# Row-wise log-sum-exp on one core: another middle range check, another division of the rows, 17 loads for 18

## The chip, the cores and the metric

The kernel runs on one core of a Trainium2 chip. The core has a tensor engine (PE), a vector engine (VectorE, DVE in the profile), a scalar engine (ScalarE, ACT), a general engine (GpSimd, POOL) and a queue engine (SyncE, SP) that issues transfers here. The metric is the time of one execution on the device in microseconds; lower is better. The time before the change is 162.31, the median of three runs (162.27 to 162.44).

## The reference

The input `x` is 32 x 512 x 1024 in 32-bit floats, drawn from a normal distribution. For each of the 16,384 rows of 1024 values the logarithm of the sum of exponentials is wanted:

```python
def reference(x):
    max_x = np.max(x, axis=-1, keepdims=True)
    return (max_x.squeeze(-1) + np.log(np.sum(np.exp(x - max_x), axis=-1))).astype(np.float32)
```

The input is 67.1 MB, the output 64 KB.

## The kernel before

Each of the 128 partitions takes 128 rows (112 from the first part of `x`, 16 from the rest), so "a row" below means one row of 1024 values on every partition at once. The kernel sums `exp(x)` without taking the maximum off. At the end it checks that every sum lies in a safe range (`LOW` 1e-15, total below `HIGH` 1e15). Only if not, a second, slow branch computes everything again with the maximum; on this input that branch is not entered.

**The list.** `LOADS` (line 23) is the plan, written out by hand. Each entry is one transfer: its size in rows, which may be a fraction, and how the rows that are complete with it are summed. SP issues the transfers in this order into `ring`, a buffer of 48 rows; a transfer into a part of the ring that was used waits until the engine that read it last is done (`load`, L132). ScalarE takes the exponential of each load in place (L213), in pieces when an entry has several parts.

**The kinds of rows.**
- `R`: VectorE reduces whole rows, several in one instruction (L224).
- `T`: VectorE adds the two halves of one row with `scalar_tensor_tensor`, whose accumulator gives the sum (`add_halves`, L156). It reads two inputs of 512 elements, one instruction and one accumulator read for each row.
- `G`: POOL adds the second half of the rows to the first (a fold, L219); later VectorE reduces the 512 elements left (`sum_folded`, L148). `H` says that the waiting folds are summed here; otherwise they are summed at the end of the entry.
- `a` and `b`: the last row comes in two pieces. `a` is summed by halves like `T`; `b` is summed by ScalarE itself, by the accumulator of its exponential (L208).
- `L`: ScalarE takes the logarithm of the first 112 sums (L199), which SP stores early (L245).
- `C`: the middle range check over the columns of `sumexp` filled so far (`check`, L163 and L167), with two matmuls that start the count in PSUM (L173, L174).

**The order.** Each engine has one queue, in the order in which the loop over `LOADS` writes it. Engines wait for each other by counting semaphores (`Counted`). `addr_align` (L186) stands on VectorE's queue ahead of the load number `ALIGNED` (15, counted from 0) and pads its instructions with empty ones up to an address boundary.

**The end.** When VectorE has its last sum and ScalarE the sum of `b`, two branches run. ScalarE takes the logarithm of 15 more columns (L249) and of the last, whose two pieces are added by the bias (L251); SP stores 16 columns (L255). Beside it VectorE checks the remaining columns (L163, L167), PE adds up over the partitions (L173, L174, L259), VectorE compares (L263), and ScalarE and VectorE read the verdict and branch.

Of the kernel before, what the change touches and what calls it, by code (L numbers as in the profile page):

```python
# [9 lines left out]
LOW, HIGH = 1e-15, 1e15  # L10
# [7 lines left out]

LOADS = [
# [4 lines left out]
]  # L26


# [23 lines left out]
def kernel(  # L52
# [5 lines left out]
    nc = tc.nc  # L58
# [43 lines left out]
    bad = sbuf("bad", 2)  # L102
    total = sbuf("total", 2)
# [31 lines left out]

    c = 0
    p = 0
    here = 0
    done_before = 0
    first_load = None  # L140
    folded = []
    summed = []

    def sum_folded():
        for c0, p0, s, at in folded:
            dve.wait(pool, at)
            half = ring[:, p0 : p0 + s * d].rearrange("p (c d) -> p c d", d=d)[:, :, 0:H]
            at = dve.did(nc.vector.reduce_sum(out=sumexp[:, c0 : c0 + s], in_=half, axis=AX.X))  # L148
            users.append((p0, p0 + s * d, dve, at))
            summed.append((c0, c0 + s, at))  # L150
        folded.clear()

    def add_halves(v, col):
        h = v.shape[-1] // 2
        lo = v[:, 0:h]
        return dve.did(nc.vector.scalar_tensor_tensor(  # L156
            out=lo, in0=lo, scalar=1.0, in1=v[:, h : 2 * h],
            op0=ALU.mult, op1=ALU.add, accum_out=sumexp[:, col : col + 1],
        ))

    def check(k, c0, c1):
        dve.wait(dve, dve.n)
        dve.did(nc.vector.scalar_tensor_tensor(  # L163
            out=clamped[:, c0:c1], in0=sumexp[:, c0:c1], scalar=LOW, in1=sumexp[:, c0:c1],
            op0=ALU.max, op1=ALU.not_equal, accum_out=bad[:, k : k + 1],
        ))
        at = dve.did(nc.vector.reduce_sum(  # L167
            out=total[:, k : k + 1], in_=sumexp[:, c0:c1], axis=AX.X
        ))
        if k == 0:  # L170
            pe.wait(pool, constants)
        pe.wait(dve, at)
        pe.did(nc.tensor.matmul(count, lhsT=bad[:, k : k + 1], rhs=far, start=k == 0, stop=False))  # L173
        pe.did(nc.tensor.matmul(count, lhsT=ones, rhs=total[:, k : k + 1], start=False, stop=False))  # L174

    for i, (size, parts) in enumerate(loads):
        if here + size > RING * d:
            assert here == p
            p = here = 0
        dma = load(i, here, done_before, size)  # L180
        first_load = first_load or dma.ins
        end = here + size
        done_before += size
        act.wait(landed[i], 16)
        if i == ALIGNED:
            nc.vector.addr_align(128)  # L186
        for k, part in enumerate(parts):
            if part[0][0] == "H":
                sum_folded()
                continue  # L190
            if part[0][0] == "C":
                sum_folded()
                checked = c
                check(0, 0, c)
                continue
            if part[0][0] == "L":
                assert c >= W
                act.wait(dve, max(at for c0, _, at in summed if c0 < W))
                ln_early = act.did(nc.scalar.activation(  # L199
                    out=res[:, 0:W], in_=sumexp[:, 0:W], func=AF.Ln  # L200
                ))
                continue
            rows = sum(s for how, s in part if how in "RTG")
            more = any(q[0][0] not in "HLC" for q in parts[k + 1 :])
            upto = p + rows * d if more else end
            v = ring[:, here:upto]
            if part[-1][0] == "b":
                last = act.did(nc.scalar.activation(  # L208
                    out=v, in_=v, func=AF.Exp, accum_out=sumexp[:, NC : NC + 1]
                ))  # L210
                here = upto
                continue
            at = act.did(nc.scalar.activation(out=v, in_=v, func=AF.Exp))  # L213
            here = upto
            for how, s in part:
                rows = ring[:, p : p + s * d].rearrange("p (c d) -> p c d", d=d)
                if how == "G":
                    pool.wait(act, at)
                    folded.append((c, p, s, pool.did(nc.gpsimd.tensor_tensor(  # L219
                        out=rows[:, :, 0:H], in0=rows[:, :, 0:H], in1=rows[:, :, H:d], op=ALU.add,  # L220
                    ))))
                elif how == "R":
                    dve.wait(act, at)
                    users.append((p, p + s * d, dve, dve.did(nc.vector.reduce_sum(  # L224
                        out=sumexp[:, c : c + s], in_=rows, axis=AX.X
                    ))))
# [12 lines left out]
                p += s * d  # L239
        sum_folded()  # L240
        assert here == end
    assert c == LAST
    assert sorted(q for c0, c1, _ in summed for q in range(c0, c1)) == list(range(NC))
# [5 lines left out]
    act.did(nc.scalar.activation(out=res[:, W:LAST], in_=sumexp[:, W:LAST], func=AF.Ln))  # L249
    act.wait(act, last)  # L250
    ln_last = act.did(nc.scalar.activation(  # L251
        out=res[:, LAST:NC], in_=sumexp[:, NC : NC + 1], func=AF.Ln, bias=sumexp[:, LAST:NC]
    ))
    sp.wait(act, ln_last)
    nc.sync.dma_start(out=out_rest, in_=res[:, W:NC]).then_inc(stored, 16)  # L255

    check(1, checked, NC)
    pe.wait(act, last)
    at = pe.did(nc.tensor.matmul(  # L259
        count, lhsT=ones, rhs=sumexp[:, NC : NC + 1], start=False, stop=True  # L260
    ))
    dve.wait(pe, at)
    at = dve.did(nc.vector.tensor_scalar(out=fine, in0=count, scalar1=HIGH, scalar2=None, op0=ALU.is_lt))  # L263
# [6 lines left out]
    with nc.If(all_fine < 1):  # L270
# [5 lines left out]
        for c0 in range(0, NC, RING):  # L276
            s = min(RING, NC - c0)
            v = ring[:, 0 : s * d].rearrange("p (c d) -> p c d", d=d)
# [4 lines left out]
            for c1, c2 in ((c0, edge), (edge, c0 + s)):  # L283
                if c1 == c2:
                    continue
                nc.scalar.dma_start(
                    out=ring[:, (c1 - c0) * d : (c2 - c0) * d],
                    in_=source(c1 * d, (c2 - c1) * d),
# [4 lines left out]
                out=neg, in_=v, op=ALU.max, axis=AX.X, negate=True  # L293
# [3 lines left out]
                out=v, in0=v, in1=neg[:, :, None].to_broadcast([P, s, d])  # L297
# [5 lines left out]
                out=sumexp[:, c0 : c0 + s], in_=v, axis=AX.X  # L303
# [71 lines left out]
```

## Time and profile before

| | before |
|---|---|
| median of 3 runs, us | 162.31 (162.27 to 162.44) |
| profiled execution, us | 162.29 |
| its span, us | 161.0 |
| VectorE busy | 119.1 us, 74% |
| ScalarE busy | 115.0 us, 71% |
| POOL busy | 32.4 us, 20% |
| PE busy | 0.5 us |
| HBM read | 67.11 MB, 417 GB/s over the span |

The span runs from the first to the last instruction of one profiled execution; the execution's time has 1.3 more around it. A row of the order of time begins with the start and the length in microseconds, then engine, line, operation, and output and input with their shapes; what stands in brackets is how long the engine stood idle before and what ended it. A row of the groups has the busy time in microseconds, then the mean in nanoseconds, then the idle time before. Lengths of neighbours on one engine overlap a little, so the cost of one in a busy queue is the distance between two starts.

### The profile page before, as it was taken

To read this page: it belongs to the slowest core of one execution; us is meant where nothing else is said; L and a number is where in the kernel's file an instruction comes from. 1 tells how busy PE (TensorE), PEld (TensorE's weight loads), DVE (VectorE), ACT (ScalarE), POOL (GpSimd) and SP (SyncE) were. 2 spreads that over 40 slices of the span, in tenths; PEclk is the share of its full clock that TensorE was granted. 3 is DMA by queue.
4 is the path that set the end of the run, shared out by engine and by line. 5 is a ranking of instruction groups with operands and counts; after the bars stand their busy time and mean duration, and the time that the engine had idled before them with its cause. 6 is when DMAs were issued, how large, how long until landed. Compare 5 with 4: busy or idle time off the path is not lost.

```text
span 161.0 us, 202 instructions
## 1 busy us (share of the span) xinstructions
PE 0.5 (0%) x10; PEld 0.3 (0%) x10; DVE 119.1 (74%) x48; ACT 115.0 (71%) x32; POOL 32.4 (20%) x15
## 2 busy tenths in 40 slices
PE   0000000000000000000000000000000000000000
PEld 0000000000000000000000000000000000000000
DVE  0000000019999499995999999999999999999996
ACT  3000059980799609994199938996997999799995
POOL 0000000000000000000008800006950806737700
DMA  7996996996996996996999969899997999999991
GB/s 261 521 521 261 521 521 261 521 521 261 521 521 261 521 521 261 521 521 261 495 469 469 469 294 507 378 401 469 455 455 336 448 420 450 390 435 412 425 409 33
DMA packets 2882, 67.18 MB, mean 417 GB/s; under 512 B 577, under 2 KB 577, under 8 KB 1345
## 3 DMA queue, kind: packets, MB, share of 16 engines
q1 hardware_dynamic: 2880, 67.18, 97.4%
q14 instruction: 2, 0.01, 0.0%
HBM read 67.11 MB, written 0.07 MB: 417 GB/s over the span
## 4 chain that ended last, share of the span: by engine, by line
DVE 52%; DMA 30%; ACT 12%; POOL 4%; issue 1%; DVEq 0%; PE 0%
DVE sumexp L224 38%; DMA ring<-in_x_dram 30%; ACT ring L213 12%; DVE sumexp L148 10%; POOL ring L219 4%; DVE ring L156 3%; DVE clamped L163 1%; DVEq L186 0%; DVE total L167 0%; PE count L173 0%; DVE fine L263 0%; PE count L259 0%; PE count L174 0%
## 5 line engine op out<-in xcount | busy, mean ns | idle before, releaser
L213 ACT ACTIVATE ring<-ring 128x16384 f32<-128x16384 f32 (+22 forms) x26 | 112.3, 4371 | 42.5 <-DMA ring<-in_x_dram 42.4
L224 DVE TENSOR_REDUCE sumexp<-ring 128x16 f32<-128x16384 f32 (+6 forms) x10 | 96.1, 9639 | 40.0 <-ACT ring L213 40.0
L219 POOL TENSOR_TENSOR ring<-ring 128x1024 f32<-128x1024 f32 (+5 forms) x9 | 32.1, 3579 | 118.3 <-ACT ring L213 118.3
L148 DVE TENSOR_REDUCE sumexp<-ring 128x2 f32<-128x1024 f32 (+5 forms) x9 | 16.1, 1802 | 0.4 <-POOL ring L219 0.4
L156 DVE SCALAR_TENSOR_TENSOR ring<-ring 128x512 f32<-128x512 f32 (+1 forms) x11 | 6.5, 642 | 0.0
L120 ACT ACT_TABLE_LOAD x1 | 1.3, 1283 | 1.4 <-PEq L61 1.4
L163 DVE SCALAR_TENSOR_TENSOR clamped<-sumexp 128x114 f32<-128x114 f32 (+1 forms) x2 | 0.9, 462 | 0.1
L208 ACT ACTIVATE ring<-ring 128x768 f32<-128x768 f32 x1 | 0.8, 843 | 0.1
L173 PE MATMUL count<-far,bad 128*1 128x1 f32 x4 | 0.4, 163 | 159.2 <-DVE total L167 159.2
L156 DVE DVE_READ_ACCUMULATOR ring<-ring 128x1 f32 x11 | 0.8, 76 | 0.0
L173 PEld LDWEIGHTS count<-far,bad 128*1 128x1 f32 x4 | 0.2, 80 | 159.2 <-POOL ring L219 151.1
L249 ACT ACTIVATE res<-sumexp 128x15 f32<-128x15 f32 x1 | 0.2, 216 | 0.4 <-DVE ring L156 0.4
L263 DVE TENSOR_SCALAR fine<-count 1x1 int32<-1x1 f32 x1 | 0.1, 147 | 0.4 <-PE count L259 0.4
L167 DVE TENSOR_REDUCE total<-sumexp 128x1 f32<-128x114 f32 (+1 forms) x2 | 0.4, 212 | 0.0
L174 PE MATMUL count<-total,ones 128*1 128x1 f32 x4 | 0.4, 163 | 0.0
L121 POOL MEMSET ones<- 128x1 f32 x1 | 0.1, 98 | 1.0 <-POOLq L61 1.0
L199 ACT ACTIVATE res<-sumexp 128x112 f32<-128x112 f32 x1 | 0.3, 280 | 0.0
L251 ACT ACTIVATE res<-sumexp 128x1 f32<-128x1 f32 x1 | 0.3, 279 | 0.0
L174 PEld LDWEIGHTS count<-total,ones 128*1 128x1 f32 x4 | 0.2, 81 | 0.0
L259 PE MATMUL count<-sumexp,ones 128*1 128x1 f32 x2 | 0.2, 163 | 0.0
L208 ACT ACTIVATION_READ_ACCUMULATOR ring<-ring 128x1 f32 x1 | 0.2, 186 | 0.0
L163 DVE DVE_READ_ACCUMULATOR clamped<-sumexp 128x1 f32 x2 | 0.2, 79 | 0.0
(6 smaller groups left out, 0.6 us busy)
## 6 DMA issues: line engine op xcount, KB each, us to landing
ring<-in_x_dram SPq DMA_DIRECT2D x1, 7376.0 KB, 24.9
ring<-in_x_dram SPq DMA_DIRECT2D x1, 5936.0 KB, 19.6
ring<-in_x_dram SPq DMA_DIRECT2D x1, 4768.0 KB, 16.4
ring<-in_x_dram SPq DMA_DIRECT2D x1, 3520.0 KB, 15.1
ring<-in_x_dram SPq DMA_DIRECT2D x1, 2976.0 KB, 21.8
ring<-in_x_dram SPq DMA_DIRECT2D x1, 1792.0 KB, 27.4
ring<-in_x_dram SPq DMA_DIRECT2D x1, 1520.0 KB, 25.0
ring<-in_x_dram SPq DMA_DIRECT2D x1, 1360.0 KB, 19.2
```

The source lines that it names most:

```text
L120: nc.scalar.preload_act_table_set("natural_log_exp_and_others")
L148: at = dve.did(nc.vector.reduce_sum(out=sumexp[:, c0 : c0 + s], in_=half, axis=AX.X))
L156: return dve.did(nc.vector.scalar_tensor_tensor(out=lo, in0=lo, scalar=1.0, in1=v[:, h : 2 * h], op0=ALU.mult, op1=ALU.add, accum_out=sume ...
L163: dve.did(nc.vector.scalar_tensor_tensor(out=clamped[:, c0:c1], in0=sumexp[:, c0:c1], scalar=LOW, in1=sumexp[:, c0:c1], op0=ALU.max, op1=A ...
L167: at = dve.did(nc.vector.reduce_sum(out=total[:, k : k + 1], in_=sumexp[:, c0:c1], axis=AX.X))
L173: pe.did(nc.tensor.matmul(count, lhsT=bad[:, k : k + 1], rhs=far, start=k == 0, stop=False))
L174: pe.did(nc.tensor.matmul(count, lhsT=ones, rhs=total[:, k : k + 1], start=False, stop=False))
L199: ln_early = act.did(nc.scalar.activation(out=res[:, 0:W], in_=sumexp[:, 0:W], func=AF.Ln))
L208: last = act.did(nc.scalar.activation(out=v, in_=v, func=AF.Exp, accum_out=sumexp[:, NC : NC + 1]))
L213: at = act.did(nc.scalar.activation(out=v, in_=v, func=AF.Exp))
L219: folded.append((c, p, s, pool.did(nc.gpsimd.tensor_tensor(out=rows[:, :, 0:H], in0=rows[:, :, 0:H], in1=rows[:, :, H:d], op=ALU.add,))))
L224: users.append((p, p + s * d, dve, dve.did(nc.vector.reduce_sum(out=sumexp[:, c : c + s], in_=rows, axis=AX.X))))
```

## The change

- The list has 17 entries for 18. The first four and the first nine hold as many rows as before (64 and 112); the sizes from the fifth on differ.
- The third load is `R12+T4`: twelve rows reduced whole, four by halves. Over the whole list there are 86 `R` rows (89 before), 18 `T` rows (10) and 21 `G` rows (28) in five folds (nine).
- The new kind `A`: ScalarE takes the exponential of one row and its sum by the accumulator, one instruction for each row. Two rows of the ninth load (`G4 A2 R1`) are summed so.
- The middle check `C` is now two reductions with one input, the least and the total of the columns so far. They go into two columns of `sumexp` behind the sums (`LEAST`, `TOTAL`); `b` has its own column behind them (`REST`). The closing check reads the columns since `C` together with `LEAST`, and adds them together with `TOTAL`. PE has three matmuls at the end and none in the middle.
- `L` stands in the tenth entry, `C` in the eleventh; before, `C` stood in the tenth and `L` in the twelfth.
- `ALIGNED` stays 15, which is now the entry before the last.

```diff
 LOADS = [
-    (16, "R16"), (16, "R16"), (16, "R16"), (16, "G6 H R10"), (14.40625, "R9 G5"),
-    (11.59375, "G3 R5 R4"), (9.3125, "G3 H R6"), (6.875, "G4 R3"), (5.8125, "G2 H R4"),
-    (2.96875, "G2 C"), (3.5, "G2 H T2"), (2.65625, "G1 T2 L"), (1.46875, "T1"),
-    (1.6875, "T2"), (1.28125, "T1"), (0.9375, "T1"), (0.75, "T1+a"), (0.75, "b"),
+    (16, "R16"), (16, "R16"), (16, "R12+T4"), (16, "R11 G5"), (11.21875, "G5 H R6"),
+    (12.78125, "R7 R6"), (9.625, "R7 G2"), (8.34375, "G5 R3"), (6.03125, "G4 A2 R1"),
+    (4.53125, "R1+T3 L"), (3.28125, "T3 C"), (2.59375, "T3"), (1.875, "T2"),
+    (1.34375, "T1"), (0.96875, "T1"), (0.6875, "T1+a"), (0.71875, "b"),
 ]
...
-    sumexp = sbuf("sumexp", NC + 1)
+    LEAST, TOTAL, REST = NC, NC + 1, NC + 2
+    sumexp = sbuf("sumexp", NC + 3)
...
-    def check(k, c0, c1):
+    def check_early(c):
+        dve.wait(act, summed_by_act)
         dve.wait(dve, dve.n)
-        dve.did(nc.vector.scalar_tensor_tensor(
-            out=clamped[:, c0:c1], in0=sumexp[:, c0:c1], scalar=LOW, in1=sumexp[:, c0:c1],
-            op0=ALU.max, op1=ALU.not_equal, accum_out=bad[:, k : k + 1],
-        ))
-        at = dve.did(nc.vector.reduce_sum(
-            out=total[:, k : k + 1], in_=sumexp[:, c0:c1], axis=AX.X
-        ))
-        if k == 0:
-            pe.wait(pool, constants)
-        pe.wait(dve, at)
-        pe.did(nc.tensor.matmul(count, lhsT=bad[:, k : k + 1], rhs=far, start=k == 0, stop=False))
-        pe.did(nc.tensor.matmul(count, lhsT=ones, rhs=total[:, k : k + 1], start=False, stop=False))
+        for op, col in ((ALU.min, LEAST), (ALU.add, TOTAL)):
+            dve.did(nc.vector.tensor_reduce(
+                out=sumexp[:, col : col + 1], in_=sumexp[:, 0:c], op=op, axis=AX.X
+            ))
...
+            if part[0][0] == "A":
+                assert here == p
+                for _ in range(part[0][1]):
+                    v = ring[:, p : p + d]
+                    summed_by_act = act.did(nc.scalar.activation(
+                        out=v, in_=v, func=AF.Exp, accum_out=sumexp[:, c : c + 1]
+                    ))
+                    users.append((p, p + d, act, summed_by_act))
...
-    check(1, checked, NC)
+    dve.wait(act, summed_by_act)
+    dve.wait(dve, sums)
+    dve.did(nc.vector.scalar_tensor_tensor(
+        out=clamped[:, 0 : LEAST + 1 - checked], in0=sumexp[:, checked : LEAST + 1], scalar=LOW,
+        in1=sumexp[:, checked : LEAST + 1], op0=ALU.max, op1=ALU.not_equal, accum_out=bad,
+    ))
+    at = dve.did(nc.vector.reduce_sum(
+        out=total, in_=sumexp[:, checked : TOTAL + 1], axis=AX.X
+    ))
+    pe.wait(pool, constants)
+    pe.wait(dve, at)
+    pe.did(nc.tensor.matmul(count, lhsT=bad, rhs=far, start=True, stop=False))
+    pe.did(nc.tensor.matmul(count, lhsT=ones, rhs=total, start=False, stop=False))
```

More of the change, by code (lines that the diff above doesn't have):

```diff
@@ L98 @@
     ring = sbuf("ring", RING * d)
-    sumexp = sbuf("sumexp", NC + 1)
+    LEAST, TOTAL, REST = NC, NC + 1, NC + 2
+    sumexp = sbuf("sumexp", NC + 3)
     res = sbuf("res", NC)
     clamped = sbuf("clamped", NC)
-    bad = sbuf("bad", 2)
-    total = sbuf("total", 2)
+    bad = sbuf("bad", 1)
+    total = sbuf("total", 1)
     far = sbuf("far", 1)
@@ L142 @@
     summed = []
+    summed_by_act = 0
+    by_act = 0
     def sum_folded():
@@ L193 @@
                 checked = c
-                check(0, 0, c)
+                check_early(c)
                 continue
@@ L197 @@
                 assert c >= W
+                assert dve.seen[act.sem.num] >= summed_by_act
                 act.wait(dve, max(at for c0, _, at in summed if c0 < W))
@@ L201 @@
                 ))
+                continue
+            if part[0][0] == "A":
[6 more added lines that the diff above has]
+                    users.append((p, p + d, act, summed_by_act))
+                    by_act += 1
+                    c += 1
+                    p += d
+                    here += d
                 continue
@@ L208 @@
                 last = act.did(nc.scalar.activation(
-                    out=v, in_=v, func=AF.Exp, accum_out=sumexp[:, NC : NC + 1]
+                    out=v, in_=v, func=AF.Exp, accum_out=sumexp[:, REST : REST + 1]
                 ))
@@ L242 @@
     assert c == LAST
-    assert sorted(q for c0, c1, _ in summed for q in range(c0, c1)) == list(range(NC))
+    assert by_act + sum(c1 - c0 for c0, c1, _ in summed) == NC
     sp.wait(act, ln_early)
@@ L251 @@
     ln_last = act.did(nc.scalar.activation(
-        out=res[:, LAST:NC], in_=sumexp[:, NC : NC + 1], func=AF.Ln, bias=sumexp[:, LAST:NC]
+        out=res[:, LAST:NC], in_=sumexp[:, REST : REST + 1], func=AF.Ln, bias=sumexp[:, LAST:NC]
     ))
@@ L255 @@
     nc.sync.dma_start(out=out_rest, in_=res[:, W:NC]).then_inc(stored, 16)
-    check(1, checked, NC)
+    dve.wait(act, summed_by_act)
[11 more added lines that the diff above has]
+    pe.did(nc.tensor.matmul(count, lhsT=ones, rhs=total, start=False, stop=False))
     pe.wait(act, last)
     at = pe.did(nc.tensor.matmul(
-        count, lhsT=ones, rhs=sumexp[:, NC : NC + 1], start=False, stop=True
+        count, lhsT=ones, rhs=sumexp[:, REST : REST + 1], start=False, stop=True
     ))
```

## The prediction

> **What bounds the kernel now.** I read the chain that ended last, then busy time by stage, then the order of time at the end, then the mean durations by shape. All times are microseconds from the start of the span. The chain's shares come first:
>
> ```profile
> DVE 52%; DMA 30%; ACT 12%; POOL 4%; issue 1%; DVEq 0%; PE 0%
> ```
>
> The stages are cut at the first fold's sum, at the ninth load's landing and at the last landing. The columns are PE, PEld, DVE, ACT and POOL busy time, then the clock, the DMA share and GB/s:
>
> ```profile
> 0.00:92.02 92.02, 0.00 (x0) 0.00 (x0) 51.66 (x4) 55.02 (x6) 7.07 (x7) 1.00 0.99 427
> 92.02:138.01 45.99, 0.00 (x0) 0.00 (x0) 45.99 (x10) 39.05 (x10) 16.13 (x4) 1.00 1.00 430
> 138.01:157.75 19.74, 0.24 (x4) 0.16 (x4) 19.71 (x27) 19.63 (x14) 9.21 (x5) 1.00 0.98 408
> 157.75:161.00 3.25, 0.29 (x6) 0.18 (x6) 1.70 (x10) 1.33 (x4) 0.00 (x0) 1.00 0.04 5
> ```
>
> The DMA never rests before 157.75, and from 92.02 VectorE does not either (45.99 of 45.99, 19.71 of 19.74). So there are two bounds, and the end shows by how much they differ:
>
> ```profile
> 157.75 0.84 ACT L208 ACTIVATE ring<-ring 128x768 f32<-128x768 f32 x1
> 158.14 0.68 DVE L156 SCALAR_TENSOR_TENSOR ring<-ring 128x512 f32<-128x512 f32 x1
> 158.50 0.19 ACT L208 ACTIVATION_READ_ACCUMULATOR ring<-ring 128x1 f32 x1
> 158.75 0.28 DVE L156 SCALAR_TENSOR_TENSOR ring<-ring 128x128 f32<-128x128 f32 x1
> 158.97 0.07 DVE L156 DVE_READ_ACCUMULATOR ring<-ring 128x1 f32 x1
> 159.07 0.22 ACT L249 ACTIVATE res<-sumexp 128x15 f32<-128x15 f32 x1 [0.39 <-DVE ring L156]
> 159.07 0.17 DVE L163 SCALAR_TENSOR_TENSOR clamped<-sumexp 128x14 f32<-128x14 f32 x1
> 159.50 0.34 SPq L255 DMA_DIRECT2D out_dram<-res  x1
> 159.72 0.15 DVE L263 TENSOR_SCALAR fine<-count 1x1 int32<-1x1 f32 x1 [0.38 <-PE count L259]
> ```
>
> ScalarE has finished the last load at 158.69 and waits 0.39 for VectorE's last sum. That sum starts both branches of the end: the closing logarithms with the last store, and the closing range check. After 159.07 nothing in either branch changes length (PE still has its three closing matmuls), so what the change is worth is how much earlier than 159.07 those two instructions start. With VectorE out of the way, ScalarE could start at about 158.72: 0.35, plus what the last landing moves.
>
> **The loads.** ScalarE started at once on landing three times, which gives the landings:
>
> ```profile
> 21.80 13.86 ACT L213 ACTIVATE ring<-ring 128x16384 f32<-128x16384 f32 x1 [19.07 <-DMA ring<-in_x_dram]
> ...
> 79.85 13.95 ACT L213 ACTIVATE ring<-ring 128x6144 f32<-128x6144 f32 x2 [5.48 <-DMA ring<-in_x_dram]
> ...
> 138.01 1.75 ACT L213 ACTIVATE ring<-ring 128x1856 f32<-128x1856 f32 x1 [0.91 <-DMA ring<-in_x_dram]
> ```
>
> Three loads of 16 rows took 58.05, so 1.2094 a row. From 138.01 to 157.75 sixteen rows in nine loads took 19.74, where 16 x 1.2094 is 19.35: 0.043 more for each load. In both kernels the first nine loads hold 112 rows, so load 9 (of the new 17) still lands at 138.01. The eight after it take 19.35 + 8 x 0.043 = 19.69 and the last lands at 157.70, 0.05 earlier. The DMA must not run dry for that. The tightest row is
>
> ```profile
> ring<-in_x_dram SPq DMA_DIRECT2D x1, 4768.0 KB, 16.4
> ```
>
> whose own transfer takes 9.31 x 1.2094 = 11.3, so it was issued 5.1 before its turn. In the new list the tightest is the sixth load, which waits for the twelve rows of the third: issued at about 87.4 for a turn at 93.4, six to spare. No wait of SP becomes tight.
>
> **VectorE.** Its prices:
>
> ```profile
> L224 DVE TENSOR_REDUCE sumexp<-ring 128x16 f32<-128x16384 f32 x3 | 51.7, 17219 | 40.0 <-ACT ring L213 40.0
> L224 DVE TENSOR_REDUCE sumexp<-ring 128x4 f32<-128x4096 f32 x2 | 8.8, 4409 | 0.0
> L148 DVE TENSOR_REDUCE sumexp<-ring 128x5 f32<-128x2560 f32 x1 | 2.8, 2808 | 0.0
> L219 POOL TENSOR_TENSOR ring<-ring 128x2560 f32<-128x2560 f32 x1 | 5.6, 5624 | 17.9 <-ACT ring L213 17.9
> L219 POOL TENSOR_TENSOR ring<-ring 128x2048 f32<-128x2048 f32 x1 | 4.5, 4537 | 5.5 <-ACT ring L213 5.5
> ```
>
> A row reduced whole costs (17.219 - 4.409) / 12 = 1.067, with about 0.06 for each instruction once its tail overlaps the next; a folded row half of that, 0.533. A row by halves (T) is 0.61, from the starts of the last two sums above (158.14, 158.75). POOL's fold is 1.09 a row.
>
> Four rows of the third load by halves save 4 x (1.067 - 0.61) = 1.8 there:
>
> ```profile
> 74.40 17.22 DVE L224 TENSOR_REDUCE sumexp<-ring 128x16 f32<-128x16384 f32 x1 [2.13 <-ACT ring L213]
> ...
> 92.02 3.35 DVE L148 TENSOR_REDUCE sumexp<-ring 128x6 f32<-128x3072 f32 x1 [0.40 <-POOL ring L219]
> ```
>
> The twelve end at 74.40 + 12.86 = 87.26, the four at 89.71. Load 4 now begins with eleven whole rows, whose exp ends at 79.85 + 9.59 = 89.44, so VectorE goes on at 89.71 without POOL, where before it waited until 92.02. That is 2.3 earlier. What is left for it then: 42 whole rows in 8 instructions 45.3, 21 folded rows in 5 instructions 11.5, 14 rows by halves 8.6, the last piece 0.2, the middle check 0.4: 66.0. From 89.71 to the last landing's 157.70 plus 0.9 are 68.9. So VectorE gets about 2.9 of idle time where it had none, and the end passes to the loads and ScalarE. Its stalls: about 0.8 for the second five-row fold (93.8 + 2 x 5.62 = 105.0, VectorE free at 104.3), 0.7 for the sixth load's exp, 0.5 for the eighth's.
>
> The middle check cost this:
>
> ```profile
> 150.05 0.75 DVE L163 SCALAR_TENSOR_TENSOR clamped<-sumexp 128x114 f32<-128x114 f32 x1
> 150.73 0.08 DVE L163 DVE_READ_ACCUMULATOR clamped<-sumexp 128x1 f32 x1
> 150.73 0.26 DVE L167 TENSOR_REDUCE total<-sumexp 128x1 f32<-128x114 f32 x1
> 150.91 1.20 DVE L148 TENSOR_REDUCE sumexp<-ring 128x2 f32<-128x1024 f32 x1
> ```
>
> From 150.05 to 150.91 is 0.86; two reductions of 119 columns by the third row are 2 x 0.18 = 0.36, 0.5 less. Even at the first row's 0.68 apiece (1.36) they would lie in the gap before the next load's exp (VectorE free at about 153.1, that exp over at 154.8). Two early PE matmuls go; PE stood idle 8 after them, so they are worth nothing.
>
> **ScalarE.** This is the engine that gets more: two rows with its own sums, and the early logarithm two loads sooner. The cost of an instruction beside its elements:
>
> ```profile
> 151.61 0.28 ACT L199 ACTIVATE res<-sumexp 128x112 f32<-128x112 f32 x1
> 151.80 1.44 ACT L213 ACTIVATE ring<-ring 128x1504 f32<-128x1504 f32 x1
> 153.15 1.63 ACT L213 ACTIVATE ring<-ring 128x1728 f32<-128x1728 f32 x1
> 154.68 1.28 ACT L213 ACTIVATE ring<-ring 128x1312 f32<-128x1312 f32 x1
> ```
>
> 1728 elements at 1/1.2 ns are 1.44, and the next starts 1.53 later: 0.09 back to back; 0.11 after a pause (157.75 to 158.50 for 768 elements, 0.64). The result is usable 0.2 after the elements. Unknown is how long the accumulator's read holds the queue, for nothing followed it at once: its row has 0.19, and the least is 0. Neighbours overlap by 0.09 (1504 took 1.44, its follower started after 1.35), so I take 0.09. The Trainium skill, "ScalarE: Activation LUTs", section "What ACT_TABLE_LOAD costs", states that ScalarE instructions back to back overlap by about 93 ns; by that the read would hold the queue 0.09 and the sum stand as it does, and the rows above agree for plain exps, while no row shows it for the read.
>
> From 138.01, the start of each instruction: exp 3104 at 138.01; the two summing rows at 140.71 and 141.75 (0.853 + 0.09 + 0.09 each); exp 1024 at 142.79; exp 4640 at 143.73 (landed 143.53); logarithm at 147.69, which also needs the four-row fold's sum: fold from 140.82 to 145.36, sum 2.3, usable at 147.68, so there is nothing to spare; then exp 3360 at 147.88 (landed 147.54), 2656 at 150.77 (150.72), 1920 at 153.08 (153.03), 1376 at 154.77 (154.70), 992 at 156.01 (155.91), 704 at 156.93 (156.79), and the last, 736, at 157.72 (157.70). ScalarE trails each landing by 0.05 to 0.3 and catches up. The last exp's sum is there at 157.72 + 0.613 + 0.11 + 0.19 = 158.63. VectorE gets the 704 at 156.93 + 0.587 + 0.2 = 157.72: one row to 158.35, a piece of 144 to 158.56, its read to 158.64. Both branches start at 158.67, 0.40 earlier than 159.07. One more thing stands on VectorE's queue, the padding of `addr_align`:
>
> ```profile
> 156.07 0.02 DVEq L186
> ...
> 156.87 0.02 DVEq L186
> ```
>
> It ran 0.8 long under two sums. Now it comes after the 992's row, which is dispatched at 157.06, and ahead of the 704's: at its old length it would end at 157.9, 0.15 past the exp it should wait for. The code ahead of it has grown by six instructions (and eight more accumulator reads), and the padding fills up to a fixed boundary, so it should be shorter and hidden: I take 0, with 0.15 as the far end. Held 0.19 by each read, the chain is 0.19 later up to the 704 and the branches start at 158.86, 0.21 earlier; held 0, the logarithm's wait on the fold keeps the 0.40.
>
> **The sum.** The last six landings lie 0.02 to 0.14 ahead of the starts they feed, so a landing 0.1 late goes nearly through; I take 0.35 of the 0.40. The profiled execution took 162.29 (span 161.0); 162.29 - 0.35 = **161.94**. The median shown, 162.31, is 0.02 above that execution.
>
> **Rivals.**
> 1. ScalarE takes VectorE's place: the reads hold it the full 0.19, or the fold's sum frees the early logarithm 0.2 later, or the padding's 0.15 shows. For it speaks that ScalarE already worked 19.63 of 19.74 in that stage; against it that it caught up with every small load. 162.29 - 0.21 = 162.08, within 0.2%.
> 2. The new sizes land later. What one load adds beside its rows is known as a mean alone. At twice 0.043 the eight add 0.34 more and the last lands at 158.04: 162.29 - 0.35 + 0.34 = 162.28; at 0 the last lands at 157.36 and ScalarE's own chain, which ends its 704 at 157.61, keeps all but 0.09 of that. Against: the sizes are of the same kind as those that gave the mean.
> 3. Slower: the early logarithm, now ahead of seven exps instead of six, blocks ScalarE while it waits for the four-row fold's sum. Each 1.0 of delay is 1.0 at the end, since nothing behind it has slack. 0.35 late (sum at 148.03) eats the gain, 0.7 late passes 0.2% on the wrong side, 1.0 late gives 162.29 - 0.35 + 1.0 = 162.94. For it: fold, sum and logarithm meet within 0.02 in the walk. Against: POOL is idle for 0.5 before that fold and VectorE for 0.1 before its sum, so neither brings a delay along.
> 4. Slower too: a row by halves beside a fold. The middle check above, with two inputs, took 0.75 for 114 columns and 0.17 for 14 at the end; POOL was folding during the first alone. The Trainium skill, "SBUF — State Buffer", section "SBUF: two separate sides", says that a VectorE instruction with two inputs and a GpSimd one that reads exclude each other for their whole length. Here the rows by halves would wait for a fold's end, but they stand at 87.3 to 89.7, before the first fold (93.8), and from 149.0 on, 3.6 after the last. Only a fold 3.6 late makes it cost, 1.0 for each further 1.0: 4.6 late gives 162.9.
>
> **How the numbers follow.** The forecast 0.52, ScalarE in the way 0.24, later landings 0.11, the early logarithm 0.11, the fold beside halves 0.02. 0.2% is 0.32, about what a measurement of this kernel can tell from no change; the forecast is just beyond it, rivals 1 and 2 are within, 3 and 4 slower: 0.52, 0.35, 0.13. The forecast's own range is 161.85 to 161.99; the whole goes from 161.82 (0.40 and a little on the landings) to 162.35, which holds rivals 1 and 2 and leaves the slower ones out.
>
> **What would show it.** After: VectorE starts its first eleven-row reduction near 89.7; it idles about 2 to 3 between 100 and 157; the two small reductions of the check take 0.3 each; the early logarithm starts near 147.7 without a wait above 0.2; the last landing is near 157.70; the closing logarithm starts within 0.1 of the accumulator read's end. Wrong it is if VectorE is still busy without a gap to the end, if ScalarE's last exp starts more than 0.1 after its landing, or if the early logarithm waits.

## The result and the profile after

| | before | after |
|---|---|---|
| median, us (22 runs each, same chips) | 162.37 (162.22 to 162.63) | 162.13 (161.95 to 162.38) |
| ratio after/before, 95% interval | | 0.9984 (0.9978 to 0.9991) |
| profiled execution, span | 162.29, 161.0 | 162.08, 160.7 |
| VectorE, ScalarE, POOL busy | 119.1, 115.0, 32.4 | 117.0, 114.6, 24.1 |

The change makes the kernel 0.24 faster, by the interval 0.15 to 0.36. That is a real gain; its middle is smaller than the 0.35 forecast, which lies near the upper end of the interval. A second measurement of the same kernel (after_again, 11 runs) gave a ratio of 0.9981 (0.9972 to 0.9990).

The chain of work that ended last has changed hands, from VectorE 52% to this:

```profile
DMA 44%; ACT 34%; DVE 13%; POOL 7%; issue 1%; PE 0%; DVEq 0%; SPq 0%
```

Busy time by stage of the kernel after, cut where VectorE begins the eleven rows, at the ninth load and at the start of the last exp; columns as in the prediction:

```profile
0.00:89.80 89.80, 0.00 (x0) 0.00 (x0) 49.76 (x10) 52.70 (x6) 0.34 (x6) 1.00 1.00 431
89.80:138.07 48.27, 0.00 (x0) 0.00 (x0) 46.62 (x10) 40.90 (x10) 16.89 (x4) 1.00 0.98 425
138.07:157.75 19.68, 0.00 (x0) 0.00 (x0) 19.16 (x32) 19.68 (x15) 6.85 (x2) 1.00 0.96 404
```

VectorE, which had no gap after 92.02, is now idle for 1.65 in the second stage and 0.52 in the third. ScalarE is the engine without a gap in the third: 19.68 of 19.68. The order of time at the end:

```profile
157.75 0.80 ACT L221 ACTIVATE ring<-ring 128x736 f32<-128x736 f32 x1
157.81 0.08 DVE L162 DVE_READ_ACCUMULATOR ring<-ring 128x1 f32 x1
157.90 0.69 DVE L162 SCALAR_TENSOR_TENSOR ring<-ring 128x512 f32<-128x512 f32 x1
158.46 0.19 ACT L221 ACTIVATION_READ_ACCUMULATOR ring<-ring 128x1 f32 x1
158.52 0.30 DVE L162 SCALAR_TENSOR_TENSOR ring<-ring 128x144 f32<-128x144 f32 x1
...
158.86 0.21 ACT L262 ACTIVATE res<-sumexp 128x15 f32<-128x15 f32 x1 [0.22 <-DVE ring L162]
158.87 0.17 DVE L272 SCALAR_TENSOR_TENSOR clamped<-sumexp 128x10 f32<-128x10 f32 x1
...
159.27 0.19 PE L281 MATMUL count<-far,bad 128*1 128x1 f32 x2 [159.27 <-DVE total L276]
159.29 0.34 SPq L268 DMA_DIRECT2D out_dram<-res  x1
159.59 0.15 DVE L288 TENSOR_SCALAR fine<-count 1x1 int32<-1x1 f32 x1 [0.47 <-PE count L284]
```

The closing logarithm starts at 158.86 instead of 159.07. One thing has to be taken off before executions are compared: when the first load lands differs from one execution to the next, and everything behind shifts with it. The first exp of this profile:

```profile
21.92 13.86 ACT L226 ACTIVATE ring<-ring 128x16384 f32<-128x16384 f32 x1 [19.19 <-DMA ring<-in_x_dram]
```

Before it started at 21.80; over the profiles of this study it (21.917 here, 21.804 before) lies between 21.73 and 22.21, which is wider than the effect. So from here on the **closing distance** is the start of the closing logarithm less the start of the first exp. It was 159.07 - 21.80 = 137.27 before and is 158.864 - 21.917 = 136.95 after (136.96 in after_again): 0.32 shorter. It comes from one profiled execution of each kernel, so a few hundredths of it are no finding by themselves.

### The profile page after: what moved, and what is told of

The parts are those of the page before. It is cut to its first block, busy times and chain, and to the rows that moved or that the text cites. A ratio compares the mean times of both kernels' runs of the same rounds, so it can differ in the third digit from the quotient of the medians.

```text
span 160.7 us, 187 instructions
## 1 busy us (share of the span) xinstructions
PE 0.3 (0%) x6; PEld 0.2 (0%) x6; DVE 117.0 (73%) x60; ACT 114.6 (71%) x32; POOL 24.1 (15%) x11
## 4 chain that ended last, share of the span: by engine, by line
DMA 44%; ACT 34%; DVE 13%; POOL 7%; issue 1%; PE 0%; DVEq 0%; SPq 0%
DMA ring<-in_x_dram 44%; ACT ring L226 32%; DVE sumexp L237 11%; POOL ring L232 7%; DVE sumexp L154 2%; ACT ring L207 1%; DVE ring L162 1%; ACT res L199 0%; PE count L281 0%; DVE clamped L272 0%; DVE fine L288 0%; DVE total L276 0%; DVEq L185 0%; PE count L284 0%; PE count L282 0%
## 5 line engine op out<-in xcount | busy, mean ns | idle before, releaser
L226 ACT ACTIVATE ring<-ring 128x16384 f32<-128x16384 f32 (+18 forms) x22 | 109.9, 5052 | 43.0 <-DMA ring<-in_x_dram 43.0
L237 DVE TENSOR_REDUCE sumexp<-ring 128x16 f32<-128x16384 f32 (+6 forms) x11 | 93.2, 8489 | 41.1 <-ACT ring L226 41.0
L232 POOL TENSOR_TENSOR ring<-ring 128x2560 f32<-128x2560 f32 (+2 forms) x5 | 23.7, 4756 | 120.1 <-ACT ring L226 120.1
L154 DVE TENSOR_REDUCE sumexp<-ring 128x5 f32<-128x2560 f32 (+2 forms) x5 | 11.9, 2388 | 0.9 <-POOL ring L232 0.8
L162 DVE SCALAR_TENSOR_TENSOR ring<-ring 128x512 f32<-128x512 f32 (+1 forms) x19 | 11.7, 668 | 0.2
L207 ACT ACTIVATE ring<-ring 128x1024 f32<-128x1024 f32 x2 | 2.1, 1040 | 0.0
L162 DVE DVE_READ_ACCUMULATOR ring<-ring 128x1 f32 x19 | 1.6, 83 | 0.0
L221 ACT ACTIVATE ring<-ring 128x736 f32<-128x736 f32 x1 | 0.8, 801 | 0.0
L171 DVE TENSOR_REDUCE sumexp<-sumexp 128x1 f32<-128x119 f32 x2 | 0.5, 272 | 0.0
```

Source lines behind the costliest of these rows:

```text
L162: return dve.did(nc.vector.scalar_tensor_tensor(out=lo, in0=lo, scalar=1.0, in1=v[:, h : 2 * h], op0=ALU.mult, op1=ALU.add, accum_out=sume ...
L171: dve.did(nc.vector.tensor_reduce(out=sumexp[:, col : col + 1], in_=sumexp[:, 0:c], op=op, axis=AX.X))
L207: summed_by_act = act.did(nc.scalar.activation(out=v, in_=v, func=AF.Exp, accum_out=sumexp[:, c : c + 1]))
L221: last = act.did(nc.scalar.activation(out=v, in_=v, func=AF.Exp, accum_out=sumexp[:, REST : REST + 1]))
L232: folded.append((c, p, s, pool.did(nc.gpsimd.tensor_tensor(out=rows[:, :, 0:H], in0=rows[:, :, 0:H], in1=rows[:, :, H:d], op=ALU.add,))))
```

## The experiments

All kernels start from the kernel after; each changes what its diff shows and computes everything the reference asks for. Ratios are against before on the same chip. A time is the median of ten or eleven executions; the four kernels with a ratio above 1 ran four times each.

| run | time | before beside it | ratio (95%) | closing distance |
|---|---|---|---|---|
| check_alone | 162.30 | 162.43 | 0.9992 (0.9983 to 1.0001) | 137.13 |
| old_check | 162.11 | 162.43 | 0.9982 (0.9973 to 0.9991) | 136.92 |
| no_halves_third | 163.26 | 162.43 | 1.0061 (1.0045 to 1.0076) | 138.03 |
| whole_in_two | 162.03 | 162.38 | 0.9979 (0.9969 to 0.9989) | 136.92 |
| no_scalar_rows | 164.15 | 162.43 | 1.0105 (1.0089 to 1.0120) | 138.89 |
| no_scalar_rows_late_log | 163.41 | 162.38 | 1.0065 (1.0048 to 1.0082) | 138.25 |
| halves_beside_fold | 166.83 | 162.38 | 1.0275 (1.0258 to 1.0292) | 141.69 |
| no_padding | 162.19 | 162.38 | 0.9996 (0.9985 to 1.0006) | 136.92 |
| after_again | 162.04 | 162.38 | 0.9981 (0.9972 to 0.9990) | 136.96 |
| tuned | 161.88 | 162.38 | 0.9974 (0.9964 to 0.9983) | 136.80 |

### The middle check: alone, and taken back

check_alone puts the list of before into the kernel after, so that of the changes only the new middle check (and the closing check that goes with it) stays. Its first five loads are those of before too; from the sixth load on the list changes so:

```diff
-    (12.78125, "R7 R6"), (9.625, "R7 G2"), (8.34375, "G5 R3"), (6.03125, "G4 A2 R1"),
-    (4.53125, "R1+T3 L"), (3.28125, "T3 C"), (2.59375, "T3"), (1.875, "T2"),
-    (1.34375, "T1"), (0.96875, "T1"), (0.6875, "T1+a"), (0.71875, "b"),
+    (11.59375, "G3 R5 R4"), (9.3125, "G3 H R6"), (6.875, "G4 R3"), (5.8125, "G2 H R4"),
+    (2.96875, "G2 C"), (3.5, "G2 H T2"), (2.65625, "G1 T2 L"), (1.46875, "T1"),
+    (1.6875, "T2"), (1.28125, "T1"), (0.9375, "T1"), (0.75, "T1+a"), (0.75, "b"),
```

> The list of before (18 loads, no T rows in the third load, no ScalarE sums) with the new middle check alone. My theory: in before the check stood from 150.05 to 150.91 and the next folded sum could have started at 150.68, when its fold was done, so the new check brings VectorE 0.23 forward; nothing else in the tail changes, the closing logarithm starts 137.06 after the first exp (before 137.27, after 136.95), and the time is about 0.2 below before: two thirds of the whole change. Rival (the new list carries the gain, the check is hidden): the closing logarithm stays at 137.27 and the time within 0.05 of before. Second rival (every part counts by the VectorE time it saves): 0.5 below before.

The closing distance fell to 137.13, 0.14 instead of 0.21 below before; the time fell 0.13, and its interval just reaches no change. The middle check of this run in the order of time:

```profile
150.34 0.45 DVE L171 TENSOR_REDUCE sumexp<-sumexp 128x1 f32<-128x114 f32 x2
150.98 1.22 DVE L154 TENSOR_REDUCE sumexp<-ring 128x2 f32<-128x1024 f32 x1 [0.19 <-POOL ring L232]
```

The next folded sum now waits 0.19 for its fold, as the theory has it, and starts at 150.98 - 22.09 = 128.89 after the first exp; before it was 150.91 - 21.80 = 129.11. Of the 0.22 won there, 0.06 goes again at the padding (below) and the rest in hundredths on the way. So by the profiles the new check alone is worth a little under half of the whole change, not two thirds.

old_check is the other way round, the new list with the old check in the middle:

```diff
-        for op, col in ((ALU.min, LEAST), (ALU.add, TOTAL)):
-            dve.did(nc.vector.tensor_reduce(
-                out=sumexp[:, col : col + 1], in_=sumexp[:, 0:c], op=op, axis=AX.X
-            ))
+        dve.did(nc.vector.scalar_tensor_tensor(
+            out=clamped[:, c0:c1], in0=sumexp[:, c0:c1], scalar=LOW, in1=sumexp[:, c0:c1],
+            op0=ALU.max, op1=ALU.not_equal, accum_out=bad[:, k : k + 1],
+        ))
+        at = dve.did(nc.vector.reduce_sum(out=total[:, k : k + 1], in_=sumexp[:, c0:c1], axis=AX.X))
...
+        pe.did(nc.tensor.matmul(count, lhsT=bad[:, k : k + 1], rhs=far, start=k == 0, stop=False))
+        pe.did(nc.tensor.matmul(count, lhsT=ones, rhs=total[:, k : k + 1], start=False, stop=False))
```

> The list of after with the middle check of before (two inputs, PE matmuls in the middle). My theory: VectorE has idle time around the check now, so the time is that of after within 0.05 (0.24 below before). What the check itself costs tells two readings of the 0.75 of before apart. If it was waiting for a POOL fold that ran beside it, the two-input instruction over 119 columns takes about 0.2 here, where no fold runs. If it costs by the column (5.8 ns each, from 0.75 for 114 and 0.17 for 14), it takes about 0.7 and the check 0.9 in all; even then it fits the gap and the end stays.

The closing distance is 136.92, that of after. The check:

```profile
152.94 0.28 DVE L169 SCALAR_TENSOR_TENSOR clamped<-sumexp 128x119 f32<-128x119 f32 x1
153.15 0.08 DVE L169 DVE_READ_ACCUMULATOR clamped<-sumexp 128x1 f32 x1
153.15 0.27 DVE L173 TENSOR_REDUCE total<-sumexp 128x1 f32<-128x119 f32 x1
153.34 0.68 DVE L162 SCALAR_TENSOR_TENSOR ring<-ring 128x512 f32<-128x512 f32 x1
```

With no fold beside it the instruction takes 0.28 over 119 columns, where before it took 0.75 over 114 (150.05 to 150.80), in the midst of three folds in a row:

```profile
145.97 5.95 POOL L219 TENSOR_TENSOR ring<-ring 128x1024 f32<-128x1024 f32 x3 [3.77 <-ACT ring L213]
```

So it was not the columns: it had waited for the fold. In either form the check costs about 0.4 there (0.40 old, 0.38 new). The two halves of the change overlap: the list alone brings 0.35, the check alone 0.14, both together 0.32. The 0.03 between the first and the last is what the padding costs in after (below); here it costs nothing.

### Four rows by halves in the third load

```diff
-    (16, "R16"), (16, "R16"), (16, "R12+T4"), (16, "R11 G5"), (11.21875, "G5 H R6"),
+    (16, "R16"), (16, "R16"), (16, "R16"), (16, "R11 G5"), (11.21875, "G5 H R6"),
```

> After with the third load summed whole again (16 rows, none by halves). My theory: VectorE starts the eleven rows of the fourth load 1.85 later, at about 91.7, its idle time before 145 shrinks by that much, and the end stays within 0.05 of after. Rival (VectorE's work counts wherever it stands): 1.85 later, 163.98.

Neither reading holds: the closing distance grew by 1.08. The two causes can be read off. The sixth load, whose exp has 6944 elements, in this run and after it in the kernel after:

```profile
109.60 5.99 ACT L226 ACTIVATE ring<-ring 128x6944 f32<-128x6944 f32 x1 [5.93 <-DMA ring<-in_x_dram]
```
```profile
108.96 5.99 ACT L226 ACTIVATE ring<-ring 128x6944 f32<-128x6944 f32 x1 [5.30 <-DMA ring<-in_x_dram]
```

One instruction over sixteen rows lets the ring go only when all are summed, so SP issued the sixth load at 91.75 instead of 87.47. Its turn came at 93.50, when the fifth had landed, as in after. 1.75 ahead was not enough: it landed 0.64 later. In the trace its first packets took 2.0 to 2.8, where those of after took 1.9; behind them both kernels load at the same pace. The profile counts the DMA engines as busy there too, so that the queue had run dry is a reading of these times. The other part shows at the end of this run:

```profile
158.48 0.82 ACT L221 ACTIVATE ring<-ring 128x736 f32<-128x736 f32 x1
158.53 0.08 DVE L162 DVE_READ_ACCUMULATOR ring<-ring 128x1 f32 x1
158.99 0.69 DVE L162 SCALAR_TENSOR_TENSOR ring<-ring 128x512 f32<-128x512 f32 x1 [0.38 <-ACT ring L226]
```

The exp that the last whole row waits for ended at 157.79 + 0.77 = 158.56, and the sum began at 158.99. Between them lies the padding, 13 empty instructions here (5 in after), the last at 158.52. To separate VectorE's own delay from these two, whole_in_two sums the same rows whole in two instructions and moves the padding away:

```diff
-ALIGNED = 15
+ALIGNED = 13
...
-    (16, "R16"), (16, "R16"), (16, "R12+T4"), (16, "R11 G5"), (11.21875, "G5 H R6"),
+    (16, "R16"), (16, "R16"), (16, "R12+R4"), (16, "R11 G5"), (11.21875, "G5 H R6"),
```

> Again the third load summed whole, but in two instructions (12 and 4 rows), so that the sixth load waits for the twelve rows as in after; the padding stands two loads earlier (ALIGNED 13), where VectorE has sums in hand. The earlier run lost 0.64 to the DMA, which ran dry before the sixth load, and 0.43 to the padding. My theory: without those two the 1.85 that VectorE loses are idle time, the last load lands as in after, the closing logarithm starts 136.95 after the first exp (within 0.05) and the time is that of after within 0.1. Rival: VectorE's own delay was part of the loss, and 0.3 or more stays.

136.92: nothing is left of the loss. The end is that of no_padding (below), the kernel after without its padding, to the hundredth. VectorE's 1.8 in the third load is worth nothing to the end. What matters there is that the twelve rows are released by an instruction of their own.

### The two rows on ScalarE, and the early logarithm

```diff
-    (6.03125, "G4 A2 R1"),
+    (6.03125, "G4 R3"),
```

> After with the two rows of the ninth load summed by VectorE instead of ScalarE (G4 R3 for G4 A2 R1): VectorE has 2.13 more, ScalarE 0.19 less. Three readings. If VectorE's idle time of about 2.9 takes it up, the time stays that of after, or is 0.1 less for ScalarE's relief. If VectorE is pushed to the end by what its remaining idle time does not cover, about 1.4 more. My theory, the early logarithm: the three rows end at 147.4 instead of 145.3, the fold's sum at 149.7, ScalarE waits about 2 for it ahead of the logarithm, and nothing behind has slack: the closing logarithm starts 2.0 later and the time is about 164.1.

The closing distance is 1.95 longer, the time 164.15. The logarithm stood exactly where the theory put it:

```profile
147.75 2.27 DVE L154 TENSOR_REDUCE sumexp<-ring 128x4 f32<-128x2048 f32 x1
149.94 1.21 DVE L237 TENSOR_REDUCE sumexp<-ring 128x1 f32<-128x1024 f32 x1
150.06 0.30 ACT L199 ACTIVATE res<-sumexp 128x112 f32<-128x112 f32 x1 [2.12 <-DVE sumexp L154]
```

From the first exp it starts at 127.85 (125.90 in after): 1.95 late there, 1.95 late at the end. Is the logarithm the cause or only a witness? The next run moves it out of the way:

```diff
-    (4.53125, "R1+T3 L"), (3.28125, "T3 C"), (2.59375, "T3"), (1.875, "T2"),
+    (4.53125, "R1+T3"), (3.28125, "T3 C"), (2.59375, "T3 L"), (1.875, "T2"),
```

together with `"G4 R3"`.

> The run without ScalarE sums (G4 R3), with the early logarithm two loads later (behind the twelfth load's exp). There the closing logarithm came 138.89 after the first exp, 1.95 later than in after. My theory was that the logarithm's wait carried that: with it out of the way ScalarE follows the landings again (last exp within 0.1 of its landing) and only what VectorE's idle time cannot take up stays, 1.4: the closing logarithm 138.35 after the first exp, the time 0.55 below that run. If the logarithm carried nothing, no change; if all, the time of after.

ScalarE no longer waits, its last exp starts 135.89 after the first (135.83 in after), and yet the closing distance is only 0.64 shorter, 1.31 longer than in after. So the theory was half right, though its 1.4 for what would stay was close: 0.64 of the loss was the logarithm holding ScalarE, and behind it stood 1.31 of VectorE's own work, which comes to light only when the first limit is gone. The closing row shows who is awaited:

```profile
160.18 0.21 ACT L262 ACTIVATE res<-sumexp 128x15 f32<-128x15 f32 x1 [1.47 <-DVE ring L162]
```

VectorE's idle time helped little because most of it (1.65 of 2.17 by the stages above) lies ahead of the ninth load. There it is still 1.65 in this run; of the 0.52 behind, 0.16 is left.

### Rows by halves beside a fold

```diff
-    (8.34375, "G5 R3"),
+    (8.34375, "G5 T3"),
```

> After with the three whole rows of the eighth load summed by halves (G5 T3 for G5 R3), with two inputs, while POOL folds five rows from 134.8 to 140.4. VectorE would have 1.4 less to do. If two-input instructions and folds exclude each other: the first of the three, ready at 138.2, stands until 140.4 (2.2 longer than 0.68), the four-row fold is pushed back or pushes the others back, and the early logarithm, which waits for that fold's sum, delays the end by 1.2 to 5. If they do not: each takes 0.68 at once, the three are done at 140.1, and the time is that of after.

Less work for VectorE, and the end 4.74 later. VectorE and POOL in the order of time, and the early logarithm on ScalarE:

```profile
134.80 5.62 POOL L232 TENSOR_TENSOR ring<-ring 128x2560 f32<-128x2560 f32 x1 [3.19 <-ACT ring L226]
...
138.23 2.74 DVE L162 SCALAR_TENSOR_TENSOR ring<-ring 128x512 f32<-128x512 f32 x1 [0.47 <-ACT ring L226]
...
140.91 0.68 DVE L162 SCALAR_TENSOR_TENSOR ring<-ring 128x512 f32<-128x512 f32 x1
140.97 5.01 POOL L232 TENSOR_TENSOR ring<-ring 128x2048 f32<-128x2048 f32 x1 [0.55 <-ACT ring L226]
...
141.52 5.01 DVE L162 SCALAR_TENSOR_TENSOR ring<-ring 128x512 f32<-128x512 f32 x1
...
152.62 0.30 ACT L199 ACTIVATE res<-sumexp 128x112 f32<-128x112 f32 x1 [4.74 <-DVE sumexp L154]
```

The first sum by halves stands until the fold is over (138.23 to 140.91). The second has the way to itself, and the next fold waits for it: 5.01 instead of 4.54. The third waits for all of that fold. The sum of the folded rows comes behind it, and the early logarithm stands 4.74 waiting for that sum: the loss at the end. The Trainium skill, "SBUF — State Buffer", section "SBUF: two separate sides", says that such a pair excludes each other for the whole instruction, whoever starts first; this trace agrees in both directions, with 2.74 and 5.01 for an instruction of 0.68.

### The padding

```diff
-ALIGNED = 15
+ALIGNED = 99
```

> After without the padding on VectorE's queue. In all runs so far the first instruction behind the padding starts 0.48 after the last empty one or later, and an instruction fetch of 8 KB follows 1.15 after. My theory: the 0.48 belongs to the crossing of the address boundary, which now comes five instructions later, in the closing check: the closing logarithm starts as in after or 0.02 earlier, but the closing check takes 0.3 to 0.45 longer from its first instruction to PE, and the time is 0.2 to 0.4 above after. Rival: the 0.48 belongs to the empty instructions, and without them the time is that of after.

In the profiled execution (162.10) the rival holds: without the padding nothing in the closing check takes longer, and the closing distance is 136.92.

```profile
157.91 0.69 DVE L162 SCALAR_TENSOR_TENSOR ring<-ring 128x512 f32<-128x512 f32 x1
...
158.87 0.21 ACT L262 ACTIVATE res<-sumexp 128x15 f32<-128x15 f32 x1 [0.20 <-DVE ring L162]
158.87 0.17 DVE L272 SCALAR_TENSOR_TENSOR clamped<-sumexp 128x10 f32<-128x10 f32 x1
```

There the 0.48 belongs to the empty instructions. Wherever the next instruction waited for nothing else, it started 0.48 after the last of them: 157.422 and 157.899 in after, 158.516 and 158.992 in no_halves_third. In after that cost 0.02 to 0.03. The times do not settle the theory, though. Six of the ten executions took 161.98 to 162.20, four took 162.49 to 162.62, and no other kernel here has such a gap among its times; the profiled execution is one of the six. The four lie 0.47 above the six on average, near the 0.2 to 0.4 of the theory, but none of them was profiled, so what they met stays open. They are why the ratio (0.9985 to 1.0006) is less good than the closing distance.

### Other sizes

The prediction's row prices fitted the kernel after well enough to choose sizes by them. In after the exp of 704 started 0.31 after its load had landed and the last one 0.08.

```diff
-ALIGNED = 15
+ALIGNED = 13
...
-    (16, "R16"), (16, "R16"), (16, "R12+T4"), (16, "R11 G5"), (11.21875, "G5 H R6"),
-    (12.78125, "R7 R6"), (9.625, "R7 G2"), (8.34375, "G5 R3"), (6.03125, "G4 A2 R1"),
-    (4.53125, "R1+T3 L"), (3.28125, "T3 C"), (2.59375, "T3"), (1.875, "T2"),
-    (1.34375, "T1"), (0.96875, "T1"), (0.6875, "T1+a"), (0.71875, "b"),
+    (16, "R16"), (16, "R16"), (16, "R12+T4"), (16, "R11 G5"), (11.75, "G5 H R6"),
+    (12.25, "R7 R6"), (10.65625, "R7 G2"), (7.65625, "G5 R3"), (5.6875, "G4 A2 R1"),
+    (4.5625, "R1+T3 L"), (3.46875, "T3 C"), (2.375, "T3"), (1.84375, "T2"),
+    (1.3125, "T1"), (0.96875, "T1"), (0.75, "T1+a"), (0.71875, "b"),
```

> The changed kernel itself, unaltered, on the same chip as the next run, as its measure: 0.24 below before (0.15 to 0.36), the closing logarithm 136.95 after the first exp within 0.03.

> The list of after with other sizes from the fifth load on, chosen by walking the engines through the list with the row prices of the prediction so that the 704 and the last exp start as soon as they land, and the padding two loads earlier. In after the 704 started 0.31 after its landing and the last exp 0.08. Walk: the closing logarithm 0.08 earlier than in after, 136.87 after the first exp, the time 0.08 less. Rival: sizes a few hundredths apart land differently from what 0.043 a load says, and the gain is within 0.03 of nothing.

after_again came out as expected: a closing distance of 136.96 and a gain of 0.31 (0.16 to 0.45). The end of tuned:

```profile
157.71 0.82 ACT L221 ACTIVATE ring<-ring 128x736 f32<-128x736 f32 x1
...
158.44 0.19 ACT L221 ACTIVATION_READ_ACCUMULATOR ring<-ring 128x1 f32 x1
158.55 0.08 DVE L162 DVE_READ_ACCUMULATOR ring<-ring 128x1 f32 x1
158.66 0.21 ACT L262 ACTIVATE res<-sumexp 128x15 f32<-128x15 f32 x1
```

The last exp starts 0.02 after its landing, and ScalarE and VectorE finish within 0.02 of each other, so the closing logarithm waits for neither. The closing distance is 136.80, 0.16 below after_again, and so is the time (161.88 beside 162.04). That is twice the 0.08 expected. By no_padding 0.03 of the 0.16 is the padding's; where the surplus comes from is not shown. Against before the ratio is 0.9974 (0.9964 to 0.9983). The intervals of the two overlap, so that tuned beats after rests on the profiles as much as on the times. It has the shortest time and closing distance here.

## Why the prediction was right, point by point

- **The number.** The measured 162.13 lies within the whole range, 161.82 to 162.35, and above the forecast's own, 161.85 to 161.99: 161.94 was 0.19 too low. Of this, 0.08 is the start, for before took 162.37 over 22 runs and not the 162.29 from which the 0.35 was taken off; 0.11 is the gain, 0.24 for 0.35. In the profiled execution 161.94 became 162.08: 0.11 is the later first exp, chance of the execution, and 0.03 is the end. In the times the gain, 0.16%, is also below the prediction's own line of 0.2%, on the side to which it gave a chance of 0.35 and not of 0.52; the 22 runs told it from nothing all the same. So the mechanism held better than the number, and the range was wide enough to hold two rivals.
- **Which engine bounds the kernel.** Right. VectorE bound it by a few tenths over the loads; with VectorE relieved, ScalarE and the loads do. The gain stayed below 0.4 although VectorE's busy time fell by 2.1. No run takes back singly the fewer folds, the sizes or the load left out, so how much of the list's 0.35 each of them brings is not shown.
- **The loads.** Right in size: load 9 landed at 138.04, the last at 157.67, so the eight took 19.64 against the 19.69 forecast, and the last landing came 0.17 earlier after the first exp than before, where 0.05 was forecast. No load came late. The sixth load's issue was forecast well (87.47 for 87.4). What the prediction missed is what the third load's new form is good for: it priced the four rows by halves by VectorE's time, which proved worth nothing, while cutting the sixteen rows into separate instructions is what issues the sixth load in time.
- **VectorE.** It began the eleven rows at 89.80 (forecast 89.71, the first exp being 0.11 later). From there to its last sum it had 2.2 idle where 2.9 was forecast: it was busy for 66.9 instead of 66.0. The middle check took 153.00 to 153.38, the forecast 0.36 and 0.02 more.
- **ScalarE.** The unknown, what the accumulator's read holds, came out where the prediction took it:

```profile
140.75 1.04 ACT L207 ACTIVATE ring<-ring 128x1024 f32<-128x1024 f32 x1
...
141.70 0.19 ACT L207 ACTIVATION_READ_ACCUMULATOR ring<-ring 128x1 f32 x1
141.79 1.04 ACT L207 ACTIVATE ring<-ring 128x1024 f32<-128x1024 f32 x1
...
147.81 0.30 ACT L199 ACTIVATE res<-sumexp 128x112 f32<-128x112 f32 x1
```

  From one summing row to the next are 1.04, 0.09 of it the read. The Trainium skill, "ScalarE: Activation LUTs", section "What ACT_TABLE_LOAD costs", states that back-to-back ACTIVATEs overlap by about 93 ns. It says nothing of the read there; this trace has the same overlap for it (0.19 long, the next instruction 0.09 after its start). The logarithm started at 147.81, the forecast 147.69 and the 0.11 of the first exp.
- **The end.** Here a term was small by 0.08. The walk gave 158.67, with the first exp's 0.11 it is 158.78, and it was 158.86. The exp of the 704 was done 0.01 late. The row behind it began another 0.035 late, 0.02 to 0.03 of it the padding, which the prediction had taken as 0 of at most 0.15. VectorE's last two sums make 0.03: 0.618 for the whole row, where the prediction had 0.61, and 0.229 for the piece of 144, where it had 0.21. ScalarE's last exp, on the other side, was 0.08 earlier than in the walk. The walk had the two engines finish together; in the trace VectorE is the later one by 0.2. So the 0.05 that the forecast took off the walk's 0.40 for late landings was lost elsewhere: the landings came early, and the end cost 0.08. That 0.32 lies so near 0.35 is in part luck.
- **The signs.** All but one came. The closing logarithm was to start within 0.1 of the end of the accumulator's read (158.64), and started 0.22 behind it: it waited for VectorE's last sum. That sum hangs on the exp of the 704, which started 0.31 after its load had landed, for ScalarE had no gap from the ninth load on. In tuned, where the exp in its place starts 0.06 after its landing, the wait is gone. The last exp started 0.08 after its landing, just inside the 0.1 that would have counted against the prediction.
- **"Nothing in either branch changes length."** Not quite. The closing check takes 0.73 from its first instruction to VectorE's comparison, where it took 0.64. The run old_check has 0.63; it differs in that PE has waited for the constants before, so here PE has one wait more between the total and the first matmul. That this wait is the reason is likely and not shown by a run of its own. The store lands last, at 160.70, and SP is through with the other branch at 160.69, so the 0.09 is hidden, by 0.02.
- **Rivals.** The first (ScalarE takes VectorE's place) happened in part: ScalarE had no gap in the last stage, and its exp of the 704 came 0.31 late, but it trailed the last landing by 0.08 only. That the profiled execution took 162.08, the very figure of this rival, is chance: none of its three conditions came at the price that it named, and 0.11 of the way there is the first exp. The second did not happen: a load cost 0.036 beside its rows, not 0.043. The third had the right place and the right price: in no_scalar_rows 1.95 of delay at the early logarithm was 1.95 at the end. It left out that VectorE's own work would stand behind it. The fourth's place was clear in after (last fold over at 145.5, next row by halves at 149.0). No run made those folds late; what such a meeting costs is shown by halves_beside_fold, where it cost 4.74.

## What to carry to other kernels

Where two engines and the loads finish within a few tenths of each other, the price of an edit is the distance to the next limit, not the time that it saves on its engine; taking the edit back shows how large that distance is, and taking a second one back shows what stands behind. Cutting a long reduction in two can be worth more for the buffer it frees than for the work. Two-input instructions on VectorE are to be kept clear of POOL's folds (one meeting cost 4.74 here), and where the start of an execution varies as much as the effect, executions are to be compared from their first dependent instruction.

## What the runs showed of the hardware

- A two-input VectorE instruction and a POOL fold exclude each other, both ways: 2.74 and 5.01 for 0.68, and 5.01 for a fold of 4.54.
- After a row of empty instructions on VectorE's queue the next one started 0.48 after the last of them, in the five profiles where it waited for nothing else; in the one profile of after without them nothing was slower.
- A load issued 1.75 before its turn came 0.64 late; the same load issued 6.0 ahead came on time.
- The first exp started between 21.73 and 22.21 in twelve profiles, and the rest of the execution moved with it.
